# Ordinary tiles yield to the side streams after every 6 matmuls instead of 12, and 21 rotary products go from GpSimd to VectorE

## The chip, the cores and the metric

The kernel runs on one core of a Trainium2 chip (trn2). The metric is the device time of one execution in microseconds, as the median of several runs. Before the change it is 2300.39 us, the median of 3 runs (2296.32 to 2301.41).

## What is computed

One step of a one-layer decoder on 512 prompt rows and 8 x 4 sample rows, all in float32:

```python
h = rmsnorm(x); z = h @ w_in          # 2048 -> 15440 columns, split into the inputs of all branches
# A: a ReLU indexer picks keys per query, then softmax attention over them, with QK-norm and rotary
# B: u * (tril(W_s[g]) @ rmsnorm(v) + b[g]) in chunks of 128
# C: 4-head cross-attention into 256 memory rows
m = sigmoid(ra)*((oa*silu(ga)) @ w_pa) + sigmoid(rb)*((ob*silu(gb)) @ w_pb) + sigmoid(rc)*((oc*silu(gc)) @ w_pc)
y = x + m @ w_out
```

Rotary turns a row (x1, x2) into (x1*cos - x2*sin, x2*cos + x1*sin). For the sample rows the picked keys and values come out of a paged cache by gathered rows, and the memory rows of branch C from a cache too.

## The kernel before

The 544 rows are kept transposed as two tiles (high and low part in the matmul's float32 form), 16 blocks of 128 features by 544 rows. A weight block of 512 by 128 is loaded (SP), cast to its high part (ScalarE, whi), and its low part (wlo) is the difference, on VectorE or, where the planner finds that sooner, on GpSimd.

**Ordinary tiles** (`columns`, lines 600 to 623) compute 128 output columns: for each of the 16 blocks of features (8 in the merge) six matmuls of 272 columns, three products (high-high, high-low, low-high) for two halves of the rows. After every second block, that is after 12 matmuls, the generator yields (lines 620 and 621). **Tiles of seven products** (`Pair`, from line 503) compute two such tiles with seven half-size products in the manner of Strassen; they yield after every 6 matmuls (line 566), in the code as it stands.

**The order of all instructions is planned by the program itself.** `Flow` (lines 68 to 231) wraps every engine: `enter` (line 99) gives each instruction a planned cost and keeps a clock for each engine, for the port that VectorE and GpSimd share, and for the DMA path; `due` (line 92) is the planned time at which a tile is ready, plus 0.4 us. `run` (line 206) has one main stream, the tiles, and several side streams, each a Python generator. In every turn each side stream may take up to 6 steps as long as what it waits for is due by TensorE's planned clock; then the main stream takes one step, up to its next yield. So the yields of the tiles are the only places at which side work gets into TensorE's queue, and also the places at which the side's instructions for the other engines and their DMAs are issued. When the main stream has ended, `run` goes on until the side streams have ended too, and only then does the next stage begin.

Stages, in order: the memory keys and values (tiles of their own kind, yielding after every 3 matmuls); the stage of the input projection (line 2100), whose main stream has 41 ordinary tiles and 43 more of the merge gates (NI, line 38); a turn of 3 ordinary tiles (line 2178), beside which the sums for the seven products are made; 34 tiles in 17 pairs of seven products (line 2205); the merge of 48 ordinary tiles and two of the output (line 2341); the rest of the output in pairs (line 2357).

The side streams of the long second stage are:

- `post_stream`, which finishes the projected tiles: for the indexer's queries and keys `rope_rows` (line 1065), for attention's queries and keys `norm_rope` (line 1142). Each has one product on GpSimd (lines 1072 and 1157). `rope_rows` runs nine times (8 of 128 rows, 1 of 64), `norm_rope` twelve times;
- `att_stream`: the scores of the sample indexer and the prompt indexer (tile qsp), memory attention, mixing, attention of the prompt;
- `prompt_choice` and `sample_choice`, the top keys by repeated MAX8 and replacement on VectorE, which step only when VectorE's planned queue is short (`idle`, line 1493);
- `cross_stream` (line 2018): dots of sample queries with cached memory keys on VectorE (tiles kc and qbc), softmax, and products with memory values;
- `sample_stream`: `sample_choice`, and when the cross stream has ended `sample_work` (line 1917): norms, a loop of 64 steps of dots between gathered keys (kgat) and queries (qbc) on VectorE, softmax, and a loop of 16 (line 1995), two of its steps for each round of four sample rows. A step has 8 matmuls of gathered values (v), issued four gathers at a time on GpSimd one step ahead; the second step of a round adds 8 matmuls with the new values (hold) and hands over to `out_features` (line 1904): a copy of the sum by ScalarE (oc), four transposes, and copies by VectorE (hold).

In the profile nearly all instructions carry line 61, that of the wrapper of the engines; they are told apart by the names of their tiles.

Of the kernel before, what the change touches and what calls it, by code (L numbers as in the profile page):

```python
# [67 lines left out]
class Flow:  # L68
# [23 lines left out]
    def due(self, *aps):  # L92
        return max(self.ready.get(a.tensor.name, 0.0) for a in aps) + SLACK
# [141 lines left out]
def decoder_step(  # L235
# [9 lines left out]
    V, S, G, PE, SP = (Engine(flow, e, k) for e, k in (  # L245
        (nc.vector, "dve"), (nc.scalar, "act"), (nc.gpsimd, "pool"), (nc.tensor, "pe"), (nc.sync, "sp")))
# [44 lines left out]
    def sm(shape, name, dt=F32, bufs=None):  # L291
        return flow.tile(small, shape, dt, name, bufs=bufs)
# [31 lines left out]
    def rsqrt(ss, n, p, w, name="rsq"):  # L324

        v, i, y, t = (sm([128, 8], name + x, dt, bufs=2)[:p, :w]
                      for x, dt in (("v", F32), ("i", I32), ("y", F32), ("t", F32)))
        V.tensor_scalar(v, ss, 1.0 / n, EPS, op0=OP.mult, op1=OP.add)
        V.tensor_scalar(i, v.bitcast(I32), 1, None, op0=OP.logical_shift_right)
        V.tensor_scalar(i, i, -1.0, 1597463007.0, op0=OP.mult, op1=OP.add)  # L330
        cur = i.bitcast(F32)
        for _ in range(3):
            V.tensor_mul(t, cur, cur)
            V.scalar_tensor_tensor(t, t, -0.5, v, op0=OP.mult, op1=OP.mult)
            V.scalar_tensor_tensor(y, t, 1.5, cur, op0=OP.add, op1=OP.mult)
            cur = y
        return y
# [20 lines left out]
    class Ring:  # L358
# [28 lines left out]
        def done(self, key):  # L387
            self.free.add(key)
# [211 lines left out]
    def columns(w, c0, m, kts, rhs, done, cond=None, ready=None, over=None):  # L600

        n = PW // 128
        parts = [(w[h * n * 128:(h + 1) * n * 128, c0:c0 + m].rearrange("(k p) c -> p k c", p=128), n, m)
                 for h in range(kts // n)]

        def emit(z, h, hl):
            for kk in range(n):
                kt = h * n + kk
                if ready and not ready(kt)():
                    yield ready(kt)  # L610
                xh, xl = rhs(kt)
                if ready:
                    yield due(xl)
                for wt, xt in ((0, 0), (0, 1), (1, 0)):
                    for a in range(2):
                        PE.matmul(z[:m, a, :TH], hl[wt][:, kk, :], (xh, xl)[xt][:, a * TH:(a + 1) * TH],
                                  start=(kt == 0 and wt + xt == 0), stop=(kt == kts - 1 and wt == 1))
                if over:
                    over()
                if kk % 2 == 1:  # L620
                    yield

        return Unit(parts, emit, lambda z: done(z[:, :, :TH]), cond)

# [390 lines left out]
    def TP_(name="tp", dt=F32):  # L1015
        return flow.tile(mpool["tp"], [128, T], dt, name, tag="tp", bufs=4)
# [24 lines left out]
    def v4(ap, a=4):  # L1041
        return ap[:, :512].rearrange("p (a b) -> p a b", a=a)
# [22 lines left out]
    def rope_rows(src, blk, cos, sin, p):  # L1065

        sw = TP_("sw")
        for b in range(p // blk):
            o, i = b * blk, (b ^ 1) * blk
            S.copy(sw[o:o + blk], src[i:i + blk])  # L1070
        V.tensor_mul(src[:p], src[:p], cos[:p])
        G.tensor_mul(sw[:p], sw[:p], sin[:p])
        yield due(sw)
        V.tensor_add(src[:p], src[:p], sw[:p])

# [9 lines left out]
    def prompt_tr(src, n=128):  # L1085

        tp = yield from psum("pp")
        for t in range(4):
            tr(tp[:, t * n:(t + 1) * n], src[:n, t * 128:(t + 1) * 128])
        yield due(tp)  # L1090
        return tp[:, :4 * n].rearrange("p (t c) -> p t c", t=4)

    def job_qi(zc, m):
        yield due(zc)
        yield from rope_rows(zc, 32, tab["cosi"], tab["sini"], 128)
        yield due(zc)
        SP.dma_start(qi_d[m * 128:(m + 1) * 128, :], zc)
        live[0] -= 1
        if m == 7:
            flags["qi"] = 1  # L1100

    def job_ki(zc):
        yield due(zc)
        wi = TP_("wi")
        S.activation(wi[:16], zc[64:80], AF.Identity, scale=0.03125)
        yield from rope_rows(zc, 32, tab["cosi"], tab["sini"], 64)
        V.tensor_copy(zc[64:128], zc[:64])
        split_from(kih, kil, zc)
        tp = yield from psum("pp")
        for t in range(4):  # L1110
            tr(tp[:, t * 16:(t + 1) * 16], wi[:16, t * 128:(t + 1) * 128])
        tr(tp[:NS, 64:80], wi[:16, TP:])
        yield due(tp)
        V.tensor_copy(wT[:, :4, :], tp[:, :64].rearrange("p (t j) -> p t j", t=4))
        V.tensor_copy(wT[:NS, 4, :], tp[:NS, 64:80])
        yield due(wT)
        SP.dma_start(w_d, wT[:NS, 4, :])
        flags["ki"] = 1
        tp = yield from prompt_tr(zc, 64)
        o = TP_("orow")  # L1120
        ov = o[:, :256].rearrange("p (t c) -> p t c", t=4)
        S.copy(ov, tp)
        yield due(o)
        SP.dma_start(kidx_prompt.rearrange("b (t p) d -> p (b t) d", p=128), ov)
        o = yield from sample_tr(zc, 64)
        SP.dma_start(kidx_sample.rearrange("b t d -> (b t) d"), o)
        live[0] -= 1
# [14 lines left out]
    def norm_rope(zc, tb):  # L1142

        tp = yield from prompt_tr(zc)
        y = v4(TP_("y"))
        S.copy(y, tp)
        ss = sm([128, 4], "ss4", bufs=2)
        for t in range(4):
            S.activation(junk_a, y[:, t, :], AF.Square, accum_out=ss[:, t:t + 1])
        yield due(ss)  # L1150
        r = rsqrt(ss, 128, 128, 4)
        for t in range(4):
            V.tensor_scalar(y[:, t, :], y[:, t, :], r[:, t:t + 1], None, op0=OP.mult)
        o, u = v4(TP_("yo")), v4(TP_("yu"))
        V.tensor_mul(o[:, :, :64], y[:, :, :64], tb[:, 0])
        V.tensor_mul(u[:, :, :64], y[:, :, 64:], tb[:, 1])
        G.tensor_mul(u[:, :, 64:], y[:, :, :64], tb[:, 3])
        V.tensor_mul(o[:, :, 64:], y[:, :, 64:], tb[:, 2])
        V.tensor_sub(o[:, :, :64], o[:, :, :64], u[:, :, :64])
        yield due(u)  # L1160
        V.tensor_add(o[:, :, 64:], o[:, :, 64:], u[:, :, 64:])
        yield due(o)
        return o
# [4 lines left out]
    def job_k(zc, g):  # L1168
        if g == 0:
            tab["q"] = yield from rope_table(g_q)  # L1170
            tab["k"] = yield from rope_table(g_k)
        yield due(zc)
        o2 = yield from sample_tr(zc)
        SP.dma_start(raw_d[:, 1024 + g * 128:1024 + (g + 1) * 128], o2)
        o = yield from norm_rope(zc, tab["k"])
        live[0] -= 1
        SP.dma_start(kcols[:, :, g * 128:(g + 1) * 128], o)
        SP.dma_start(rows4(k_d)[:, :, g * 128:(g + 1) * 128], o)
# [14 lines left out]
    def job_q(zc, h):  # L1193
        yield due(zc)
        o2 = yield from sample_tr(zc)
        SP.dma_start(raw_d[:, h * 128:(h + 1) * 128], o2)
        o = yield from norm_rope(zc, tab["q"])
        live[0] -= 1
        SP.dma_start(rows4(q_d)[:, :, h * 128:(h + 1) * 128], o)
        if h % 2:  # L1200
            flags["kvq%d" % (h // 2)] = 1
# [980 lines left out]
    def over(product):  # L2182
        flags["past" + product] = 1
# [224 lines left out]
```

## Time and profile before

| | us |
|---|---|
| median of 3 runs | 2300.39 (2296.32 to 2301.41) |
| profiled execution, its own time | 2297.85 |
| its span, first to last instruction | 2296.1 |
| TensorE busy (matmul) | 2223.4 |
| VectorE busy | 1686.7 |
| ScalarE busy | 964.5 |
| GpSimd busy | 283.8 |

The profiled execution is one run more, beside the three; its span is the part in which engines work. In the profile PE is TensorE's matmul, PEld its weight load, DVE VectorE, ACT ScalarE, POOL GpSimd, SP the queue that issues most DMAs. A busy matmul may include waiting inside a run of matmuls, so a stage in which TensorE reads as busy is not always one that is full.

### The profile page before, as it was taken

The numbers are of one execution on the slowest core, as the hardware profiler recorded it, in microseconds if no ns is written. First come the engines' busy times: TensorE is split into PE (matmuls) and PEld (weight loads), VectorE is DVE, ScalarE is ACT, GpSimd is POOL, SyncE is SP. The second block draws the span as 40 slices with busy tenths as digits, with TensorE's granted clock in tenths as the row PEclk, the third lists the DMA queues.
The fourth block names the chain that finished last, engine by engine and source line by source line (L and its number), as shares of the span: only waits on it lengthen the run. The fifth ranks groups of instructions, "written<-read, shape, count | busy, mean of one in ns | idle before, by whom it ended". The sixth has DMA issues, their size and how long they took to land. (4 is left out here: it accounts for less than half of the span.)

```text
span 2296.1 us, 46130 instructions
## 1 busy us (share of the span) xinstructions
PE 2223.4 (97%) x17057; PEld 2138.6 (93%) x17057; DVE 1686.7 (73%) x4658; ACT 964.5 (42%) x1944; POOL 283.8 (12%) x275
## 2 busy tenths in 40 slices
PE   8899999899999999999999998999999999999999
PEld 6699999899999998999999985999999999999999
DVE  7843557999889899666889514998899635567786
ACT  6544454454454432444544322444444422233443
POOL 1121220010010011001333343000000001200000
PEclk9999999999999999999999999999999999999999
DMA  7654434556556766446788776344454645444453
GB/s 245 220 173 109 124 101 112 167 147 190 164 170 197 221 196 189 137 122 180 251 272 272 221 214 173 100 127 134 128 163 143 204 135 172 143 132 136 128 158 88
DMA packets 497535, 382.17 MB, mean 166 GB/s; under 512 B 35786, under 2 KB 427068, under 8 KB 497308
## 3 DMA queue, kind: packets, MB, share of 16 engines
q1 hardware_dynamic: 485532, 341.45, 50.7%
q0 software_dynamic: 11776, 37.76, 5.0%
q8 instruction: 134, 2.20, 0.4%
q14 instruction: 93, 0.76, 0.1%
HBM read 329.81 MB, written 49.30 MB: 165 GB/s over the span
## 5 line engine op out<-in xcount | busy, mean ns | idle before, releaser
L61 PE MATMUL z<-x,whi 128*128 128x272 f32 (+1 forms) x5696 | 960.9, 291 | 0.0
L61 PEld LDWEIGHTS z<-x,whi 128*128 128x128 f32 (+1 forms) x5696 | 805.9, 188 | 19.3 <-issue 12.6
L61 DVE TENSOR_TENSOR wlo<-raw,whi 128x512 fp32r<-128x512 f32 (+1 forms) x613 | 427.0, 706 | 274.7 <-ACT whi L61 264.8
L61 ACT CAST whi<-raw 128x512 fp32r<-128x512 f32 (+1 forms) x660 | 402.8, 619 | 537.8 <-PE z L61 349.3
L61 PE MATMUL z<-x,wlo 128*128 128x272 f32 (+1 forms) x2848 | 589.8, 289 | 0.9 <-DVE wlo L61 0.9
L61 PEld LDWEIGHTS z<-x,wlo 128*128 128x128 f32 (+1 forms) x2848 | 445.5, 189 | 1.3 <-DVE wlo L61 1.3
L61 PE MATMUL zs<-x,whi 128*128 128x272 f32 x1536 | 293.5, 289 | 2.2 <-ACT whi L61 1.4
L61 PEld LDWEIGHTS zs<-x,whi 128*128 128x128 f32 x1536 | 242.6, 189 | 2.7 <-ACT whi L61 1.7
L61 PE MATMUL zs<-x,wlo 128*128 128x272 f32 x768 | 223.0, 290 | 1.3 <-DVE wlo L61 1.3
L61 ACT CAST whi<-wsum 128x512 fp32r<-128x512 f32 x192 | 119.2, 622 | 131.7 <-PE zs L61 97.3
L61 PE MATMUL zs<-oh,wlo 128*128 128x272 f32 x576 | 167.0, 290 | 1.7 <-DVE wlo L61 1.7
L61 PE MATMUL zs<-oh,whi 128*128 128x272 f32 x576 | 167.0, 290 | 0.2 <-ACT oh L61 0.2
L61 PE MATMUL zs<-ol,whi 128*128 128x272 f32 x576 | 165.6, 288 | 0.4 <-DVE ol L61 0.4
L61 PE MATMUL z<-oh,whi 128*128 128x272 f32 x768 | 159.2, 289 | 3.7 <-DVE zc L61 2.6
L61 PE MATMUL z<-ol,whi 128*128 128x272 f32 x768 | 158.8, 288 | 0.4 <-DVE ol L61 0.2
L61 PE MATMUL z<-oh,wlo 128*128 128x272 f32 x768 | 158.4, 287 | 0.0
L61 PEld LDWEIGHTS zs<-x,wlo 128*128 128x128 f32 x768 | 145.0, 189 | 1.5 <-DVE wlo L61 1.5
L61 DVE TENSOR_TENSOR wlo<-wsum,whi 128x512 fp32r<-128x512 f32 x181 | 121.5, 683 | 13.8 <-ACT whi L61 13.8
L61 POOL TENSOR_TENSOR wlo<-raw,whi 128x512 fp32r<-128x512 f32 x47 | 63.5, 1352 | 526.8 <-ACT whi L61 431.3
L61 PEld LDWEIGHTS z<-oh,whi 128*128 128x128 f32 x768 | 120.4, 188 | 4.1 <-issue 2.8
L61 PEld LDWEIGHTS z<-ol,whi 128*128 128x128 f32 x768 | 120.7, 189 | 0.8 <-DVE ol L61 0.8
L61 PEld LDWEIGHTS z<-oh,wlo 128*128 128x128 f32 x768 | 120.2, 188 | 0.0
(340 smaller groups left out, 3119.7 us busy)
## 6 DMA issues: line engine op xcount, KB each, us to landing
raw<-in_w_in_dram SPq DMA_DIRECT2D x480, 256.0 KB, 3.2
raw<-in_w_mem_kv_dram SPq DMA_DIRECT2D x64, 256.0 KB, 4.9
qbc<-cqs_d SPq DMA_DIRECT2D x64, 256.0 KB, 5.0
qbc<-qs_d SPq DMA_DIRECT2D x32, 512.0 KB, 5.6
raw<-in_w_out_dram SPq DMA_DIRECT2D x64, 256.0 KB, 2.7
kc<-in_cache_mem_k_dram SPq DMA_DIRECT2D x32, 256.0 KB, 4.5
raw<-in_w_pb_dram SPq DMA_DIRECT2D x32, 256.0 KB, 2.6
raw<-in_w_pc_dram SPq DMA_DIRECT2D x32, 256.0 KB, 2.7
```

The source lines that it names most:

```text
L61: r = f(*args, **kwargs)
```

## The change

In ordinary tiles the generator yields after every block of features, that is after every 6 matmuls, so the side streams are asked twice as often. This holds for the ordinary tiles of all stages. The two products on GpSimd in `rope_rows` and `norm_rope` are issued on VectorE instead, in the same place of the program. Since every instruction enters the planner's clocks, the order of later instructions and the choice between VectorE and GpSimd for low parts can change too.

```diff
@@ columns
                 if over:
                     over()
-                if kk % 2 == 1:
-                    yield
+                yield
@@ rope_rows
         V.tensor_mul(src[:p], src[:p], cos[:p])
-        G.tensor_mul(sw[:p], sw[:p], sin[:p])
+        V.tensor_mul(sw[:p], sw[:p], sin[:p])
         yield due(sw)
@@ norm_rope
         V.tensor_mul(u[:, :, :64], y[:, :, 64:], tb[:, 1])
-        G.tensor_mul(u[:, :, 64:], y[:, :, :64], tb[:, 3])
+        V.tensor_mul(u[:, :, 64:], y[:, :, :64], tb[:, 3])
         V.tensor_mul(o[:, :, 64:], y[:, :, 64:], tb[:, 2])
```

## Rows read from the trace of the kernel before

**Rows 1.** The page: the span, and TensorE's busy time, share and instructions.
```profile
span 2296.1 us, 46130 instructions
...
PE 2223.4 (97%) x17057; PEld 2138.6 (93%) x17057; DVE 1686.7 (73%) x4658; ACT 964.5 (42%) x1944; POOL 283.8 (12%) x275
```

**Rows 2.** Stretches: length, busy us by engine, granted clock, DMA share, GB/s.
```profile
172.00:287.00 115.00, 115.00 (x918) 113.61 (x917) 55.51 (x92) 53.20 (x105) 24.54 (x19) 1.00 0.43 117
402.00:689.00 287.00, 267.55 (x2056) 261.46 (x2055) 262.53 (x865) 133.74 (x351) 22.60 (x22) 0.98 0.59 167
1080.00:1271.00 191.00, 189.83 (x1512) 188.93 (x1511) 165.19 (x1114) 84.14 (x146) 63.47 (x59) 1.00 0.85 269
1378.30:1410.25 31.95, 25.28 (x105) 4.87 (x105) 1.88 (x13) 3.47 (x6) 19.30 (x21) 0.95 0.67 197
1410.25:1462.50 52.25, 48.24 (x378) 47.16 (x376) 47.56 (x78) 22.53 (x40) 0.00 (x0) 1.00 0.38 105
1811.00:2140.00 329.00, 322.97 (x2569) 321.66 (x2568) 178.40 (x248) 97.69 (x165) 21.86 (x17) 1.00 0.48 148
```

**Rows 3.** Waits of TensorE, 402 to 689 us: us in total, times, longest.
```profile
PE pa L61 <- DVE ph L61: 5.4, 2, 5.3
```

**Rows 4.** Timeline of TensorE after 430 us: start, length; in brackets idle before.
```profile
439.96 0.69 PE L61 MATMUL pa<-kih,qsp 128*128 128x384 f32 x1 [8.61 <-DVE qsp L61]
...
441.40 1.11 PE L61 MATMUL z<-x,whi 128*128 128x272 f32 x4
```

**Rows 5.** From 1378.3 to 1410.25 us: a wait, then one round's timeline.
```profile
PEld ps L61 <- DMA v<-in_cache_v_dram,gidx: 14.5, 14, 1.2
...
1379.34 1.04 PE L61 MATMUL ps<-hold 32*8 32x512 f32 x8
1381.14 0.66 PE L61 MATMUL ps<-ident,oc 128*128 128x128 f32 x4 [0.76 <-ACT oc L61]
1382.32 1.07 PE L61 MATMUL ps<-v,qbc 128*32 128x512 f32 x8 [0.53 <-PE ps L61]
```

**Rows 6.** Timeline of ScalarE: first, fifth and last of eight copies oc.
```profile
1315.64 0.59 ACT L61 COPY oc<-ps 128x512 f32<-128x512 f32 x1 [3.12 <-PE ps L61]
...
1380.50 0.58 ACT L61 COPY oc<-ps 128x512 f32<-128x512 f32 x1 [0.87 <-PE ps L61]
...
1409.20 0.58 ACT L61 COPY oc<-ps 128x512 f32<-128x512 f32 x1 [9.41 <-PE ps L61]
```

**Rows 7.** Timeline of TensorE in an ordinary tile, twelve matmuls apart.
```profile
1411.08 0.66 PE L61 MATMUL z<-x,whi 128*128 128x272 f32 x4
...
1412.59 0.67 PE L61 MATMUL z<-x,whi 128*128 128x272 f32 x4
```

**Rows 8.** A stretch from one round's transposes to the next's, columns as before.
```profile
1348.64:1365.97 17.33, 17.33 (x139) 14.50 (x138) 3.79 (x9) 4.71 (x8) 8.21 (x9) 1.00 0.73 216
```

**Rows 9.** A stretch, tile kgat alone: length, VectorE, GpSimd, clock, DMA share, GB/s.
```profile
1080.00:1280.90 200.90, 112.31 (x1024) 63.47 (x59) 1.00 0.86 274
```

**Rows 10.** Timeline of TensorE: the ordinary matmuls right behind four transposes.
```profile
423.05 0.74 PE L61 MATMUL z<-x,whi 128*128 128x272 f32 x4
```

**Rows 11.** The rotary tiles' instructions: ns min/median/max, first and last start.
```profile
L61 DVE TENSOR_TENSOR yo<-yo,yu x24: 409/412/421, 424.4 to 662.2; 128x256 f32<-128x256 f32 x24
L61 POOL TENSOR_TENSOR yu<-y,rtab x12: 872/901/927, 423.0 to 654.9; 128x256 f32<-128x256 f32 x12
L61 DVE TENSOR_TENSOR yu<-y,rtab x12: 946/962/967, 423.2 to 655.1; 128x256 f32<-128x256 f32 x12
...
L61 POOL TENSOR_TENSOR sw<-sw,itab x9: 1379/1897/1903, 145.2 to 241.8; 128x544 f32<-128x544 f32 x8, 64x544 f32<-64x544 f32 x1
L61 DVE TENSOR_TENSOR zc<-zc,sw x9: 706/712/718, 147.6 to 244.2; 128x544 f32<-128x544 f32 x8, 64x544 f32<-64x544 f32 x1
```

**Rows 12.** Timeline of VectorE from 183 us, beside a wide product on GpSimd.
```profile
183.03 1.84 DVE L61 TENSOR_TENSOR wlo<-raw,whi 128x512 fp32r<-128x512 f32 x1
...
185.42 0.68 DVE L61 TENSOR_TENSOR wlo<-raw,whi 128x512 fp32r<-128x512 f32 x1
```

## The prediction

> **What bounds the kernel now.** The page comes first: TensorE is busy 97% of the span [rows 1]. The change removes no matmul column, so only the stretches in which TensorE waits can give time. The table by stage says where those are [rows 2]. From 172 to 287 us and from 1080 to 1271 TensorE idles 0 and 1.2 us. From 402 to 689 it idles 19.5 us (287.00 less 267.55), and VectorE is busy for 262.53 of the 287: that stretch is VectorE's. The waits of TensorE name tiles made there, ph with 5.4 us among them [rows 3]. One stop shows the pattern: at 431 us TensorE stands still for 8.61 us for qsp, whose low half waits its turn in VectorE's queue, and its next four matmuls take 1.11 us where 0.66 is usual [rows 4]. The granted clock of the stretch, 0.98 where the quiet ones have 1.00, says the same: for a moment after such a stop the lower level (1.2 GHz) holds.
>
> The second place hides behind a busy number. The stretch from 1378.3 to 1410.25 reads 25.28 us of TensorE busy [rows 2], but it holds no ordinary tile until its last instant: that stage's tiles are used up, and TensorE serves the sample stream's value products alone, whose weight loads wait 14.5 us for gathered rows [rows 5]. The sample stream is the last to end in its stage, and what makes it end sooner shortens the kernel. ScalarE's copies give the pace of its eight rounds: under ordinary tiles four intervals take 1380.50 - 1315.64, 16.2 us each, and alone three take 1409.20 - 1380.50, 9.6 us each [rows 6].
>
> **The finer yields.** They add and remove no instruction; the order in the queues changes. Twelve matmuls of an ordinary tile take 1.51 us (1411.08 to 1412.59) [rows 7]. A side step that has become due is put in at the next yield, on average half a period late: 0.75 us before, 0.38 after. So each binding wait of a side chain gets shorter by an estimated 0.38 us. Whatever a step issues moves with it, its loads on SP and its gathers on GpSimd too.
>
> A round that moves from the tail to under ordinary tiles saves its 9.6 us there and costs TensorE what it inserts. From 1348.64 to 1365.97, 17.33 us, TensorE has 139 matmuls [rows 8], 28 of them the round's own (8 and 8 of values, 8 of hold, 4 transposes, as in the tail [rows 5]). The other 111, at 1.51/12 = 0.126 us, make 14.0, which leaves 3.4. So a round moved gains 9.6 - 3.4 = 6.2 us.
>
> How many move: (a) within a round six waits (two sets of values, the sum, its copy, the transposes, the bank) give 2.2 of 16.2 us, so the 69 us before 1378 hold 4.9 rounds instead of 4.25, +0.65. (b) The loop of 64 dots steps before it takes 200.9 us, 3.14 a step, in which its own VectorE work is 112.31 us, 1.75 a step [rows 9]. At 0.38 a step 24 us could go, but with all streams VectorE is at 165.19 of 191 us there and the DMA engines at 0.85 [rows 2]; I take a third, 8 us. (c) The softmax, the norms, the tables and the memory-value products, from 830 to 1080 us and after the loop, have some 60 waits by the code, 22 us at most; about half stand behind VectorE's queue, so 10 us. (d) The cross dots before 830 us go at VectorE's own pace: 0. The 18 us of (b) and (c) are 1.1 rounds of 16.2 us. In all 1.75 rounds, **-11 us**, bounded by 0 (each wait is really for data) and -18.6 (all three rounds).
>
> The yields also let dots and maxima into VectorE's queue sooner, ahead of what TensorE waits for. The nearest row is the 19.5 us of idle; the work stays the same, so I take **+2**, between -3 and +10 (half of that idle once more). The handover from 1410.25 to 1462.5 idles 4.0 us (52.25 less 48.24), for sums that now come a little sooner: **-1**, between -4 and 0. Cutting the side's blocks finer makes a few new seams; after four transposes the next four matmuls take 0.74 instead of 0.66 us [rows 10]; twenty of them would be 1.6, and I take 0, covered by the idle above. From 1811 to 2140, where the merge tiles get the new yields, TensorE idles 6.0 of 329 us, at the borders of stages: 0, between -1 and +1. The tiles of seven products already yield at every six: 0.
>
> **The rotary products.** GpSimd loses 12 products of 128x256 (901 ns) and 9 of 544 columns (1897 ns). VectorE gains 12 at 412 ns, 4.9 us, and 9 at 712 ns, 6.4 us [rows 11]. But VectorE's own yu, started just behind GpSimd's, takes 962 ns against the 412 of the same shape, and the wlo that follows a wide product on GpSimd takes 1.84 us against the 0.68 of the next one [rows 11, 12]. The two yu together then take some 840 ns instead of 962: 12 x -0.12 = -1.4 us in the saturated stretch, and I take **-1**, between -1.4 and +4.9. The nine wide ones lie where VectorE is busy 55.51 of 115 us and TensorE never idles [rows 2]: 0 under that cover; without it between -4.0 (9 x (0.71 + 0.68 - 1.84)) and +6.4. No new kind of wait stands in VectorE's queue: the cosine product just ahead waits for the same copies. GpSimd's queue gets shorter, and its gathers there feed a stream that is not last: 0.
>
> The Trainium skill (Perfetto Trace Analysis, Optimizing Scalar/DVE Operations) speaks against this half: where VectorE is saturated, moving work off it, even to GpSimd, may pay. By that rule taking it back costs the 4.9 us; the trace agrees about the saturation, and the row of 962 ns shows the relief given back.
>
> **Sum.** -11 + 2 - 1 - 1 = -11. The profiled execution took 2297.85 us (span 2296.1 [rows 1] and 1.75 around it), so 2286.9; the median shown stands 2.5 us above it, so 2289.4, say **2289 us**. A measurement of this kernel can tell about 0.2%, 4.6 us, from no change.
>
> **Rivals.** *Data's pace*: the sample stream is held by loads and VectorE, not by yields. For it speak the 0.85 of DMA in the loop and the gathers in the tail; against it, that a round takes 6.6 us longer under tiles than alone. Only the products and the handover are left, -2: 2298. Chance 0.16.
>
> *The added products are paid in full*: +4.9 instead of -1 between 402 and 689, 2289 + 6 = 2295, on the edge of what can be told. Against it stands the row of 962 ns. Chance 0.06. This is the cited rule's case.
>
> *VectorE backs up*, the slower side: dots and maxima let in sooner push qsp and ph back, and stops like those of 8.6 and 5.4 us come once more, 14 us, with some 4 at the lower clock. The tail, fed through the same engine, then gains one round, 6.2: 2300.4 + 18 - 6 = 2312. It decides from two added stops on. For it speaks VectorE's 91% there; against it, that no work is added. Chance 0.16.
>
> *The whole tail goes*: three rounds, -18.6, and -2: 2280. Chance 0.08.
>
> **How the numbers follow.** The forecast keeps 0.54, of which 0.03 lies within 0.2%. Faster: 0.51 + 0.08 + 0.02 of the products' case = 0.61. Same: 0.16 + 0.03 + 0.04 = 0.23. Slower: 0.16. The range runs from just past the whole tail, 2278, into the slower case, 2304 (one stop more and no round moved), and leaves out about one in ten above and less below.
>
> **What would show it.** After the change six or seven rounds lie under ordinary tiles; the stretch without tiles falls from 32 to between 10 and 20 us; the loop of dots ends some 18 us sooner; yu stands twice on VectorE near 0.42 us, and GpSimd has no product of 544. Wrong: three rounds alone as before (data's pace), or over 30 us of TensorE idle from 402 to 689 (VectorE backs up).

## The result, and the profile after

The changed kernel takes **2272.09 us** (median of four runs, 2271.11 to 2273.32), the kernel before, on the same chip at the same time, 2299.06: ratio 0.9887 with a 95% interval of 0.9874 to 0.9901, 27.0 us. The forecast said -11, and the measured time lies below the lower end of its range, 2278. The profiled run took 2271.11 us against 2297.85.

The page after, the span and the engines' busy times [rows 1]:

```profile
span 2269.3 us, 46101 instructions
...
PE 2212.1 (97%) x17057; PEld 2134.9 (94%) x17057; DVE 1679.2 (74%) x4668; ACT 962.3 (42%) x1942; POOL 269.1 (12%) x265
```

The stretches that answer to [rows 2], in their columns; the last three are moved to where the same part of the program now lies:

```profile
402.00:689.00 287.00, 276.99 (x2168) 271.90 (x2167) 266.90 (x957) 139.63 (x369) 9.90 (x9) 0.99 0.67 198
1371.00:1380.90 9.90, 7.51 (x39) 2.58 (x37) 0.74 (x2) 1.71 (x3) 1.89 (x2) 0.95 0.44 134
1380.90:1434.90 54.00, 49.27 (x377) 48.19 (x375) 47.98 (x77) 22.39 (x40) 1.31 (x1) 0.97 0.37 102
1783.00:2112.00 329.00, 323.09 (x2572) 321.78 (x2570) 177.85 (x248) 96.73 (x163) 21.90 (x17) 1.00 0.48 147
```

TensorE idles 10.0 of 287 us where VectorE is saturated, not 19.5, though VectorE has 92 instructions more there. The stretch without ordinary tiles is 8.8 us long (their last matmuls end near 1372.1), not 31.95.

ScalarE's copies of the rounds' sums [rows 6], in the timeline of the changed kernel: first, sixth, seventh and last of eight.

```profile
1268.35 0.59 ACT L61 COPY oc<-ps 128x512 f32<-128x512 f32 x1 [2.33 <-PE ps L61]
...
1352.03 0.59 ACT L61 COPY oc<-ps 128x512 f32<-128x512 f32 x1 [3.93 <-PE ps L61]
1368.55 0.59 ACT L61 COPY oc<-ps 128x512 f32<-128x512 f32 x1 [1.62 <-PE ps L61]
1379.48 0.58 ACT L61 COPY oc<-ps 128x512 f32<-128x512 f32 x1 [6.14 <-PE ps L61]
```

Seven rounds lie under ordinary tiles (five before, the fifth's copy 2 us behind them), one is alone. Under tiles a round takes (1368.55 - 1268.35)/6 = 16.7 us, not less than the 16.2 of before.

The end of the long stage moved from 1410.9 to 1381.7 us, by 29.2, and what lies behind it takes about as long as before (887.6 and 885.2 us). These 29 us are: the stretch alone 31.95 - 8.8 = 23.1 shorter; the two more rounds put some 2 x 3.4 = 6.8 us of their own matmuls under the tiles (3.4 is the prediction's estimate); and TensorE's idle time from 115 us to the last ordinary tile fell by 12.7 us, from 32.2 to 19.4 (length less TensorE's busy time, before and after):

```profile
115.00:1378.34 1263.34, 1231.19 (x9626) 1190.03 (x9624) 927.77 (x3306) 545.90 (x1189) 214.19 (x211) 0.99 0.61 179
115.00:1372.06 1257.06, 1237.65 (x9698) 1188.90 (x9699) 920.07 (x3328) 545.32 (x1190) 214.22 (x212) 1.00 0.62 184
```

What brought the rounds forward is read from the first and last starts of the sample stream's tiles. Before, in the view by tile (ns min/median/max, first and last start): the cross stream's dots, the sample search's maxima, the cross stream's last store, the dots with gathered keys.

```profile
L61 DVE SCALAR_TENSOR_TENSOR junk_v<-kc,qbc x256: 393/417/1500, 430.9 to 829.7; 128x256 bf16<-128x256 f32 x128
L61 DVE MAX8 hold<-hold x32: 1211/1224/1227, 366.9 to 925.4; 64x8 f32<-64x1028 f32 x32
L61 SPq DMA_DIRECT2D oc_d<-hold x1: 508/508/508, 943.9 to 943.9; - x1
L61 DVE SCALAR_TENSOR_TENSOR junk_v<-kgat,qbc x512: 277/286/324, 1080.0 to 1280.6; 128x128 bf16<-128x128 f32 x171
```

The same after:

```profile
L61 DVE SCALAR_TENSOR_TENSOR junk_v<-kc,qbc x256: 406/420/1523, 430.7 to 758.3; 128x256 bf16<-128x256 f32 x128
L61 DVE MAX8 hold<-hold x32: 1209/1224/1227, 357.1 to 920.3; 64x8 f32<-64x1028 f32 x32
L61 SPq DMA_DIRECT2D oc_d<-hold x1: 417/417/417, 853.9 to 853.9; - x1
L61 DVE SCALAR_TENSOR_TENSOR junk_v<-kgat,qbc x512: 277/288/360, 1049.3 to 1240.2; 128x128 bf16<-128x128 f32 x171
```

`sample_work` needs both the search and the cross stream. Before, the cross stream was last (943.9); after, it ends 90 us sooner and the search is last (922.8, the end of its index search). So the work starts 21.1 us sooner, its dots 30.7 sooner, their end 40.4, and the first value product 46.6 (1309.4 to 1262.8).

### The profile page after: what moved, and what is told of

It reads as the page before. It is cut to its first block, busy times and chain, and to the rows that moved or that the text cites. A ratio compares the mean times of both kernels' runs of the same rounds, so it can differ in the third digit from the quotient of the medians.

```text
span 2269.3 us, 46101 instructions
## 1 busy us (share of the span) xinstructions
PE 2212.1 (97%) x17057; PEld 2134.9 (94%) x17057; DVE 1679.2 (74%) x4668; ACT 962.3 (42%) x1942; POOL 269.1 (12%) x265
## 4 chain that ended last, share of the span: by engine, by line
PE 77%; DVE 14%; DMA 4%; issue 3%; ACT 2%; SPq 0%; POOL 0%; DVEq 0%; ACTq 0%; POOLq 0%
PE z L61 49%; PE zs L61 21%; PE pa L61 5%; DVE junk_v L61 2%; DVE wlo L61 2%; PE ps L61 2%; DVE selb L61 1%; DVE hold L61 1%; DMA raw<-in_w_mem_kv_dram 1%; ACT whi L61 1%; DVE sidx L61 1%; DVE m L61 1%; DMA raw<-in_w_in_dram 1%; DVE rsqt L61 1%; PE pp L61 1%
## 5 line engine op out<-in xcount | busy, mean ns | idle before, releaser
L61 DVE TENSOR_TENSOR wlo<-raw,whi 128x512 fp32r<-128x512 f32 (+1 forms) x603 | 411.5, 694 | 267.7 <-ACT whi L61 257.5
L61 POOL TENSOR_TENSOR wlo<-raw,whi 128x512 fp32r<-128x512 f32 x57 | 76.9, 1350 | 851.7 <-ACT whi L61 714.0
```

Source lines behind the costliest of these rows:

```text
L61: r = f(*args, **kwargs)
```

## Experiments

All diffs are against the kernel named; "before" is always a fresh run of it on the same chip. Three theories were stated first. **T1**: the streams have ranks. The searches stand ahead of the dots in the list of streams and step while VectorE's planned queue is at most 2.0 us ahead of TensorE (A1, A2, line 44), the cross dots and gathered dots up to 3.0 (A3). With 1.5 us between yields the queue has always run down by more than that gap of 1.0 at the next one, and the search steps in first; with 0.75 us it has not, and the dots are let in. **T2**: each wait ends half a period sooner. **T3**: the products relieve VectorE where TensorE waits for it.

**e1, the finer yields alone** (against before):

```diff
-                if kk % 2 == 1:
-                    yield
+                yield
```

> The yields after every 6 matmuls alone; the 21 rotary products stay on GpSimd. If the yields do it (theory 1: they let the cross dots pass the top-key search in VectorE's queue; theory 2: each side wait ends 0.38 us sooner), most of the 27 us stays: 2272 to 2282 us, the last cross dots near 760 us, the loop of gathered dots beginning near 1050. If the products do it (theory 3: VectorE relieved where TensorE waits for it), 2288 us or more.

2286.49 us, ratio 0.9946 (0.9929 to 0.9962): between the two forecasts, about half of the 27 us. The cross dots end near 773 us and the loop of gathered dots begins at 1054.9, much as T1 and T2 have it.

**e2, the products alone** (against before):

```diff
-        G.tensor_mul(sw[:p], sw[:p], sin[:p])
+        V.tensor_mul(sw[:p], sw[:p], sin[:p])
...
-        G.tensor_mul(u[:, :, 64:], y[:, :, :64], tb[:, 3])
+        V.tensor_mul(u[:, :, 64:], y[:, :, :64], tb[:, 3])
```

> The 21 rotary products on VectorE alone; ordinary tiles still yield after 12 matmuls. Theories 1 and 2: 2293 to 2300 us, the last cross dots still near 830 us, three rounds of value products without ordinary tiles. Theory 3: 2285 us or less, and TensorE's idle from 402 to 689 us falls from 19.5 to about 10.

2300.7 us, ratio 1.0001 (0.9991 to 1.0011), and TensorE's idle time from 402 to 689 us is 21.4 us, not 10: T3 fails for the products alone. The parts don't add: 13.3 and nothing, together 27.0. The dots and maxima of e1, then of e2:

```profile
L61 DVE SCALAR_TENSOR_TENSOR junk_v<-kc,qbc x256: 397/420/1517, 430.8 to 773.1; 128x256 bf16<-128x256 f32 x128
L61 DVE MAX8 hold<-hold x32: 1208/1223/1225, 358.0 to 929.7; 64x8 f32<-64x1028 f32 x32
```

```profile
L61 DVE SCALAR_TENSOR_TENSOR junk_v<-kc,qbc x256: 393/416/1510, 432.8 to 849.7; 128x256 bf16<-128x256 f32 x128
L61 DVE MAX8 hold<-hold x32: 1211/1223/1225, 368.0 to 920.0; 64x8 f32<-64x1028 f32 x32
```

In e2 the search ends 5 us sooner and the cross dots, which are last there, 20 us later: it looks as if the time that VectorE was given went to the stream that did not need it. (Its profiled run lay 6 us above its median.)

**e3, T1 without finer yields** (against before): a gap wider than the period.

```diff
-A1, A2, A3 = 2.0, 2.0, 3.0
+A1, A2, A3 = 1.0, 1.0, 3.0
```

> The kernel before with the top-key searches held back more: they step only with VectorE's planned queue at 1.0 us or less instead of 2.0, while the cross dots keep 3.0. The gap of 2.0 us is then wider than the 1.5 us between two yields. Theory 1 (it is gap against yield period that decides who gets VectorE): the last cross dots come down from 830 to 740 to 780 us without any finer yield, and the sample's top-key search ends later than its 928. Theory 2: the cross dots stay at 815 to 835 us. The total may go either way, since the search is starved.

2288.99 us, ratio 0.9957 (0.9941 to 0.9973). The cross dots end as early as with the whole change, and the search pays:

```profile
402.00:689.00 287.00, 276.41 (x2155) 272.40 (x2154) 263.07 (x956) 140.86 (x373) 16.30 (x17) 0.99 0.68 197
...
L61 DVE SCALAR_TENSOR_TENSOR junk_v<-kc,qbc x256: 408/421/427, 427.8 to 747.0; 128x256 bf16<-128x256 f32 x128
L61 DVE MAX8 hold<-hold x32: 1209/1217/1225, 368.2 to 962.2; 64x8 f32<-64x1028 f32 x32
```

TensorE's idle time falls to 10.6 us as well, with yields every twelve matmuls.

**e4, finer yields without the gap** (against the changed kernel):

```diff
-A1, A2, A3 = 2.0, 2.0, 3.0
+A1, A2, A3 = 3.0, 3.0, 3.0
```

> The changed kernel with no gap: the top-key searches step at a planned queue of 3.0 us as the cross dots do. Theory 1: the cross dots lose their lead and end at 810 us or later (758 in the changed kernel), the sample's search ends well before its 923. Theory 2: the cross dots stay within 10 us of 758. Total 2262 to 2282 us.

2322.97 us, ratio 1.0103 (1.0083 to 1.0123), slower than before, and far above the 2262 to 2282 expected. The order is turned round: the search ends near 742 us, and until then no cross dot begins.

```profile
L61 DVE SCALAR_TENSOR_TENSOR junk_v<-kc,qbc x256: 398/419/506, 742.5 to 972.9; 128x256 bf16<-128x256 f32 x128
L61 DVE MAX8 hold<-hold x32: 1214/1224/1225, 357.1 to 740.1; 64x8 f32<-64x1028 f32 x32
```

e3 and e4 together show T1: the gap moves the cross dots without any change of yields, and without it the finer yields lose all they gave, and more. T2 can't make either.

**e6, yields after every two matmuls** (against the changed kernel):

```diff
                 for wt, xt in ((0, 0), (0, 1), (1, 0)):
...
+                    if wt == 0:
+                        yield
```

> The changed kernel with yields after 2, 4 and 6 of every 6 matmuls instead of after 6. Theory 1 (gap of 1.0 us against the yield period): 0.75 us is already below the gap, so the cross dots keep their end within 10 us of 758 and the search within 10 of 923; the total falls by at most 6 us. Theory 2 (half a period per wait): each wait ends another 0.25 us sooner, two thirds of what 12 to 6 gave: the loop of gathered dots begins 15 us or more sooner and the total falls to 2262 or less.

2277.45 us, ratio 0.9909 (0.9893 to 0.9926). Cross dots to 756.7 us as T1 said, TensorE's idle time from 402 to 689 us down to 7.1, the search done ten us sooner; the loop of dots begins 4.8 us sooner (1044.5), not the 15 of T2. The total is 5 us above the changed kernel, outside both forecasts, though the two intervals overlap. e5 shows why.

**e5, a shorter planned gather** (against the changed kernel; it asks what sets the 16.6 us of a round):

```diff
-                start += 1.7
+                start += 0.7
```

> The changed kernel, but the planner counts 0.7 instead of 1.7 us from a gather's issue on GpSimd to its transfer; no instruction is added or removed. If the rounds of value products are paced by the planned arrival of their gathers, and not by the yields, the spacing of the copies oc under ordinary tiles falls from 16.6 to 14 to 15 us, all eight rounds or all but half a round lie under ordinary tiles, and the total falls to 2260 to 2268 us. If real data pace them, the spacing stays at 16 us or more, or TensorE waits for gathered rows under the ordinary tiles by more than 4 us in all, and the total stays at 2269 to 2276.

2272.82 us, ratio 0.988 (0.9864 to 0.9897), the same as the changed kernel. First and last copies of the eight rounds in ScalarE's timeline:

```profile
1277.78 0.59 ACT L61 COPY oc<-ps 128x512 f32<-128x512 f32 x1 [1.63 <-PE ps L61]
...
1376.54 0.59 ACT L61 COPY oc<-ps 128x512 f32<-128x512 f32 x1 [1.68 <-PE ps L61]
```

A round now takes 98.76/7 = 14.1 us, and all eight lie under tiles: the planned arrival of the gathers paces a round, not the yields. What this gives, 2.7 us at the stage's end, is lost behind the stage. TensorE's timeline at the seven products and the stretch behind its stop (granted clock third from the end), both of e5, then the timeline of the changed kernel:

```profile
1427.90 0.60 PE L61 MATMUL zs<-oh,whi 128*128 128x272 f32 x1 [5.46 <-ACT oh L61]
...
1427.90:1430.00 2.10, 1.94 (x7) 1.63 (x8) 2.07 (x3) 0.00 (x0) 0.00 (x0) 0.50 0.00 0
```

```profile
1425.48 0.39 PE L61 MATMUL zs<-oh,whi 128*128 128x272 f32 x1 [0.88 <-ACT oh L61]
```

The sums for the seven products (oh) are made beside the turn of three tiles, which takes 37 us (1379.9 to 1416.9 in e5). They come 43.8 us after the stage's end in the changed kernel (1381.7) and 48.9 in e5 (1379.0): a stop of 5.46 us, in e6 one of 7.82, with matmuls at half the clock behind it. That the changed kernel has them sooner because VectorE is nearly idle beside its last round alone (0.74 of 9.9 us, the window above) is argued, not shown.

**e7, the wide products back on GpSimd** (against the changed kernel):

```diff
-        V.tensor_mul(sw[:p], sw[:p], sin[:p])
+        G.tensor_mul(sw[:p], sw[:p], sin[:p])
```

> The finer yields and the 12 products of 128x256 on VectorE; the 9 wide ones stay on GpSimd. The wide ones lie where VectorE is half idle, so they should not count: 2270 to 2276 us, the search of the sample ending within 4 us of 923. If the wide ones matter, it comes out nearer to the 2286 of the yields alone: 2279 or more.

2270.75 us, ratio 0.9874 (0.9857 to 0.989): the wide ones count for nothing, the twelve narrow ones are the change's.

**e8, e3 with the products on VectorE** (against before; the wide product too, as in e2):

```diff
-A1, A2, A3 = 2.0, 2.0, 3.0
+A1, A2, A3 = 1.0, 1.0, 3.0
...
-        G.tensor_mul(u[:, :, 64:], y[:, :, :64], tb[:, 3])
+        V.tensor_mul(u[:, :, 64:], y[:, :, :64], tb[:, 3])
```

> Yields after 12, searches held back to 1.0 us as in the run with gap 2.0, and all 21 products on VectorE. In that run the sample's search was the last to end (963 us), as in the changed kernel. If the products count only where the search is the last (the time they free on VectorE goes to whoever steps last), the search ends 6 us or more before 963 and the total is 2278 to 2286 us, against 2289 without the products. If they count only with finer yields for another reason, nothing changes: 2287 to 2291.

2280.11 us, ratio 0.992 (0.9903 to 0.9936), 8.9 less than e3, where the search is last too:

```profile
L61 DVE SCALAR_TENSOR_TENSOR junk_v<-kc,qbc x256: 405/419/1512, 424.2 to 726.7; 128x256 bf16<-128x256 f32 x128
L61 DVE MAX8 hold<-hold x32: 1211/1224/1225, 364.8 to 956.1; 64x8 f32<-64x1028 f32 x32
```

So the products pay without finer yields too, where the search is last. That e2 gave nothing because the cross stream was last there fits both runs.

**e9, the searches planned nearer to their length** (against the changed kernel):

```diff
+            if op in ("max", "match_replace", "max_index"):
+                c += 0.09 if op == "max" else 0.16
```

> The changed kernel with one thing changed in the planner: the three operations of the top-key searches are planned longer (the 8-fold maximum by 0.09 us, the replacement and the index search by 0.16 us each). No instruction is added; only the order is planned with later ends of the searches. The question is why TensorE's idle time between 402 and 689 us fell from 19.5 us before to 10.0 after, though VectorE got finer yields and more work. Theory U (a search step that is really longer than planned lets VectorE run late against the plan, and TensorE then waits for an evacuation): with the searches planned nearer to their length, idle time of 402 to 689 us at most 6 us. Rival (the stops come from the attention's own chains, ScalarE and VectorE in turn, whatever the searches cost): 9 to 11 us as in the changed kernel. In both the planner gives the searches fewer steps per round, so that the sample's search ends later than 922.8 us, by 10 to 30 us, and with it the end of the stage (1380.9 us) by as much less what the fewer stops return: total 2275 to 2295 us.

2280.01 us, ratio 0.9913 (0.9896 to 0.9929). The total came as expected, the idle time between the two theories: 8.7 us from 402 to 689, but 0.55 from 689 to 918, where the changed kernel idles 7.1. The two stretches in e9:

```profile
402.00:689.00 287.00, 278.34 (x2167) 273.40 (x2168) 262.13 (x933) 140.46 (x366) 12.90 (x12) 0.99 0.67 190
689.00:918.00 229.00, 228.45 (x1787) 215.05 (x1786) 206.02 (x526) 84.28 (x205) 32.24 (x33) 1.00 0.64 189
```

With the searches planned longer the stops behind 689 us are gone, as theory U has it; those ahead of 689 hardly change, and their cause stays open.

**e10 and e11, a turn of four tiles**, with the planned gather of e5 and without:

```diff
-NI, NT = 43, 3
+NI, NT = 42, 4
```

> The kernel of e5 (changed kernel, planned gather shorter by 1.0 us) with 42 ordinary r tiles ahead of the stage's end and 4 in the turn after it, instead of 43 and 3. In e5 the tail was gone (all eight copies of a round beside ordinary tiles, the last at 1376.5 us), but the 7-8 us so gained were lost again behind the stage: TensorE waited 5.5 us for oh (the sums of the tokens' quarters that the seven-product stage needs) at 1422.2 us, and ran its next matmuls at half clock (0.60 us against 0.29). Theory H (the turn of 37 us is too short to cover the sums, some 49 us from 1379.0 to 1427.9): with a turn of 4 tiles (about 48 us) the stop shrinks to under 1.5 us; the ordinary tiles end some 12 us sooner (about 1367 us), so that about one round stands alone and costs up to 5 us more there; total 2264 to 2271 us, below the 2272 of the changed kernel. Rival (the sums start only when the tail's last rounds free VectorE or the pools, so they end as late as before whatever the turn's length): the stop stays at 4 us or more, or a tail of 10 us and more returns; total 2272 to 2282 us.

> The changed kernel with 42 ordinary r tiles and 4 in the turn, and the planned gather as it was: the control to e10. The ordinary tiles end 12 us sooner (about 1360 us) while the rounds keep their 16.6 us spacing, so two rounds (copies at about 1368 and 1379 us) stand alone in place of one, and the stage ends within 3 us of 1381 us with a turn that is 12 us longer behind it; less the handover's stop of 0.9 us and the half clock behind it. Theory H with the rounds paced by the planned gathers: 2277 to 2285 us, slower than the changed kernel by 5 to 12 us. Rival (the rounds are paced by the ordinary tiles' yields or by the chip's own gather, and so move with the tile that is taken away): 2268 to 2275 us.

e10: 2268.42 us, ratio 0.9867 (0.985 to 0.9883); e11: 2268.92 us, 0.9862 (0.9845 to 0.9878). Both are 3 us below the changed kernel, the lowest medians here, but the intervals overlap with its own. In e10 the stop for oh is gone, as expected: no wait of TensorE from 1360 to 1440 us is for oh, and the longest is 1.9 us. In e11 none is for oh either.

In e11 the total fell within the rival's span, not the theory's. The last three copies of its rounds:

```profile
1354.37 0.59 ACT L61 COPY oc<-ps 128x512 f32<-128x512 f32 x1 [3.93 <-PE ps L61]
1365.79 0.59 ACT L61 COPY oc<-ps 128x512 f32<-128x512 f32 x1 [5.93 <-PE ps L61]
1374.82 0.59 ACT L61 COPY oc<-ps 128x512 f32<-128x512 f32 x1 [8.44 <-PE ps L61]
```

The theory had kept the rounds at 16.6 us after the tiles were gone; alone they took 11.4 and 9.0, as the rival's rounds do. So the stage ended 5.1 us sooner (1376.6), the tile put behind it cost 5.4 there, and the spans of the two profiled runs are equal (2269.6 and 2269.3).

**e12 and e13, order and chip apart.** The 21 products act in two ways: on the chip, and through the planner, which counts a product of 256 columns on GpSimd as 256 x 0.0022 + 0.1 = 0.66 us in which VectorE's two-input operations wait, and one on VectorE as 256 x 0.00104 + 0.065 = 0.33. e12 is the changed kernel's order with the products on GpSimd, e13 the order of e1 with the products on VectorE (shown: one of the two lines of each).

```diff
-        V.tensor_mul(u[:, :, 64:], y[:, :, :64], tb[:, 3])
+        G.engine.tensor_mul(u[:, :, 64:], y[:, :, :64], tb[:, 3])
+        flow.enter("dve", "tensor_mul", (u[:, :, 64:], y[:, :, :64], tb[:, 3]), {})
```

```diff
-        G.tensor_mul(u[:, :, 64:], y[:, :, :64], tb[:, 3])
+        V.engine.tensor_mul(u[:, :, 64:], y[:, :, :64], tb[:, 3])
+        flow.enter("pool", "tensor_mul", (u[:, :, 64:], y[:, :, :64], tb[:, 3]), {})
```

> The changed kernel with its 21 products run on GpSimd as before, but entered in the planner as if they were VectorE's: the order of all other instructions is the changed kernel's. Theory C (the chip: VectorE is blocked while GpSimd multiplies, 12 products of 962 ns against 418 ns, and waits for the later halves): the gain of 14 us is lost, 2284 to 2290 us, with the sample's search ending at 928 us or later and TensorE's idle time of 402 to 689 us at 12.5 us or more. Theory O (the order: with the products planned on VectorE the planner gives the searches and dots other places): 2270 to 2276 us, search end within 3 us of 922.8 us, idle time within 1.5 us of 10.0 us.

> The kernel with finer yields alone (2286.5 us), with its 21 products run on VectorE but entered in the planner as GpSimd's: the order of all other instructions is that of finer yields alone. Theory C: 2270 to 2276 us, the search ending by 925 us, idle time of 402 to 689 us 10 to 11 us. Theory O: 2283 to 2289 us, search end within 3 us of 932 us (its last maximum began at 929.7 us), idle time 12.5 us or more. If each way gives a part, the two runs lie between and their gains add up to about 14 us.

| order planned for | run on GpSimd | run on VectorE |
|---|---|---|
| GpSimd | e1: 2286.49, 0.9946 (0.9929 to 0.9962) | e13: 2278.33, 0.9916 (0.9899 to 0.9932) |
| VectorE | e12: 2276.23, 0.9903 (0.9887 to 0.992) | changed: 2272.09, 0.9887 (0.9874 to 0.9901) |

Both ways give a part, and each run falls between its two forecasts: the chip gives 8.2 us under the one order and 4.1 under the other, the order 10.3 and 6.2. (That each pair adds up to 14.4 is arithmetic: both ways lead from e1 to the changed kernel.) The sizes are rough: an interval is some 4 us to either side, and of the four neighbours in the table only e1 and e12 have intervals that don't overlap.

The traces, one profiled run each, show where each part lies. TensorE and the other engines from 115 us to the last ordinary tile, in e1, e13 and e12 (the changed kernel's line stands with the result):

```profile
115.00:1371.41 1256.41, 1233.77 (x9652) 1190.71 (x9651) 924.64 (x3297) 549.03 (x1190) 234.69 (x230) 0.99 0.62 181
115.00:1367.21 1252.21, 1232.00 (x9654) 1190.67 (x9652) 920.22 (x3319) 548.82 (x1190) 204.77 (x202) 0.99 0.62 182
115.00:1378.56 1263.56, 1240.29 (x9705) 1189.50 (x9703) 925.15 (x3307) 545.51 (x1190) 243.90 (x240) 1.00 0.62 183
```

The chip's part lies under the tiles. With the products run on VectorE the last ordinary tile ends 4.2 us sooner (e1 to e13) and 6.5 (e12 to the changed kernel); 2.4 and 3.9 us of that are idle time of TensorE, which is T3's kind of gain. The stretch alone keeps its length: 22.9 and 22.7 us, 8.6 and 8.8. The order's part is two rounds: the stretch alone gets 14.3 us shorter (e1 to e12) and 13.9 (e13 to the changed kernel), for a last tile that ends 7.1 and 4.8 us later. The rounds start sooner because the loop of dots with gathered keys gets 15 us shorter, 191 us in the two kernels planned for VectorE, 206 in the two planned for GpSimd. The dots in e1, e13 and e12:

```profile
L61 DVE SCALAR_TENSOR_TENSOR junk_v<-kgat,qbc x512: 274/289/300, 1054.9 to 1260.5; 128x128 bf16<-128x128 f32 x171
L61 DVE SCALAR_TENSOR_TENSOR junk_v<-kgat,qbc x512: 277/287/323, 1051.1 to 1257.0; 128x128 bf16<-128x128 f32 x171
L61 DVE SCALAR_TENSOR_TENSOR junk_v<-kgat,qbc x512: 278/288/300, 1055.7 to 1246.4; 128x128 bf16<-128x128 f32 x171
```

Attention's last store comes at 1200.3 us in e1, 1196.1 in e13, 1189.7 in e12 and 1183.2 in the changed kernel, so in the kernels planned for VectorE more of the dots run without attention beside them. Why attention ends sooner in those orders is not shown.

The tile yu in e12 (line 1157 is the product itself), then in e13:

```profile
L1157 POOL TENSOR_TENSOR yu<-y,rtab x12: 837/892/962, 427.9 to 646.8; 128x256 f32<-128x256 f32 x12
L61 DVE TENSOR_TENSOR yu<-y,rtab x12: 427/962/971, 428.2 to 647.0; 128x256 f32<-128x256 f32 x12
```

```profile
L1157 DVE TENSOR_TENSOR yu<-y,rtab x12: 412/418/420, 425.5 to 637.4; 128x256 f32<-128x256 f32 x12
```

## Why the prediction was wrong

**What held.** The sample stream was rightly seen as the last of its stage. Six or seven rounds under tiles were foreseen, seven came. Two signs were undershot: 10 to 20 us alone (8.8 came) and a loop of dots that ends some 18 us sooner (40 came). *Data's pace* fell with e1, *VectorE backs up* with the idle time of 10 us; *the whole tail goes* came nearest: two of three rounds went.

**The step that failed** is the rotary products, "-1, between -1.4 and +4.9": with finer yields they give 14.4 us (e1 against the changed kernel), and alone nothing. The bound was taken from VectorE's busy time on the two yu, 12 x -0.12. That much the trace after confirms: 24 of them at 418 ns are 10.0 us, and 12 at 962 were 11.5. Two things were left out. The planner's clock is an input of the change: a product entered on another engine moves the rest of the order. The section on the change names this, but the sum has no term for it; by the table of e12 and e13 it is worth 6 to 10 us, two rounds that come under the tiles. And the chip's part, 4 to 8 us, is several times VectorE's 1.5 us of busy time; in the traces over half of it is idle time of TensorE. What turns 1.5 us in VectorE's queue into that much is not shown. The products' value also hangs on which stream is last (e2 against e8), and that the first half of the change alters this was not asked.

**The Trainium skill's rule** (Perfetto Trace Analysis, Optimizing Scalar/DVE Operations), that work may be moved off a saturated VectorE even to GpSimd, spoke for a loss of 4.9 us and fell: the way back gave 4 to 8 us on the chip alone. The Trainium skill's caution in the same section, that the two share a read port and that moving between them might not help, is what the 962 ns against 418 in e12 and e13 agree with.

**The finer yields, term by term**, are read from e1 against before, which leaves the products out. Forecast were -11 + 2 - 1 = -10, by 1.75 rounds; measured were -13.3, by about one round (the stretch alone 22.9 us instead of 32) and 9.5 us less idle time of TensorE (22.6 instead of 32.2, the lines from 115 us). That the total came near was luck. (a) "Shorter rounds, +0.65": wrong, (1358.51 - 1291.40)/4 = 16.8 us under tiles by the copies of e1 instead of 16.2, and e5 shows the planned gathers as their pace. (b) "8 us in the loop": wrong, the loop takes 205.6 us in e1 and 200.6 before. The dots in two stretches, up to attention's last store and behind it (length, VectorE, GpSimd, clock, DMA share, GB/s), before and in e1:

```profile
1080.00:1252.90 172.90, 91.38 (x832) 55.73 (x52) 1.00 0.84 265
1252.90:1280.90 28.00, 20.93 (x192) 7.74 (x8) 1.00 0.97 329
```

```profile
1054.80:1200.30 145.50, 66.96 (x608) 40.10 (x38) 1.00 0.79 241
1200.30:1260.90 60.60, 45.32 (x416) 22.52 (x22) 1.00 1.00 327
```

A step has 16 of these instructions. Beside the attention it takes 172.9/52 = 3.3 us before and 145.5/38 = 3.8 in e1; without it 28/12 = 2.3 in both. No step got faster: 14 more of the 64 run after the attention has ended, and the others are slower. (c) "10 us": more, 17. From the start of `sample_work` (943.9 before, 932.3 in e1) to the dots it takes 13.5 us less, from the dots to the values 3.5. (d) "The cross dots go at VectorE's own pace: 0" is the failed term here: their pace was set by rank, and they ended 57 us sooner at the same 0.42 us each, which put `sample_work` 11.6 us forward, until the search held it. Together 11.6 + 13.5 - 5.0 + 3.5 = 23.6 us at the first value product, 1.4 rounds.

**The gain per round**, 6.2 us: about right. The order's part shortens the stretch alone by 14 us, 1.5 rounds of 9.6, which is 9 us at that price; the stage ends 7.1 and 9.0 us sooner. **VectorE backs up, +2 (-3 to +10)**: wrong sign and beyond the bound; TensorE's idle time in that stretch fell by 6.4 us in e1 and by 9.5 with the whole change. e3 has the same fall without finer yields, which points to the searches' taking their turns later and not to the yields' length. The range's lower end, 2278, was the whole tail and little else: it left no room for 12.7 us of idle time that went under the tiles. **The handover, -1**: 4.7 us idle (54.00 less 49.27) after 4.0 before, just outside its bound. Its real size showed where the tail was gone (e5, e6). **Merge tiles, 0**: 5.9 us idle after 6.0, right. **Wide products, 0**: right (e7).

## What to carry to other kernels

Where the program plans its own order, price an edit twice: what the chip does with it, and what the planner's clock makes of the rest, and run each with the other held fixed. Before pricing relief on a shared engine, ask which stream ends last and by which threshold it gets its turn; a period between turns that crosses such a threshold reorders the streams and does more than shorten waits. When a tail goes, look at once at what it was covering.

## What the runs showed of the hardware that was not expected

A product of 128x256 on VectorE that starts just behind one on GpSimd takes 960 to 962 ns, and 418 or 419 where both are VectorE's (medians of the kernels here). That it costs the stage more than the difference of 12 such times, 6.5 us less the 5.0 that VectorE takes on, was not expected (4 to 8 us). After a stop of 5.46 us the granted clock of the next 2.1 us was 0.50, the lower level (1.2 GHz), and single matmuls of 272 columns took 0.60 us; after one of 0.88 us it was 1.00, and such a matmul took 0.39.
